# Forming the input projection of an S5 / RG-LRU layer with seven block products in place of eight

## The chip, the cores and the metric

The kernel runs on one core of one Trainium2 chip. The metric is the device time of one execution in microseconds (us). The engines are TensorE (PE in the profile, with its weight loads as PEld), VectorE (DVE), ScalarE (ACT), GpSimd (POOL) and SyncE (SP, which here only issues DMAs). The matmul accumulators lie in PSUM, in banks of 128 x 512 float32.

## The reference, cut to what matters

2048 tokens of a prompt and 128 of eight samples (2176 in all) pass through one layer of width 1024:

```python
h = rmsnorm(x, ln_g)
proj = h @ w_in                                   # 1024 -> 5120 columns
u_a, z_a, u_b, z_b, g_a, g_b = split(proj)        # 512, 512, 1024, 1024, 1024, 1024
y_a, s5_new = s5_mixer(u_a, ...)                  # complex diagonal scan, 32 groups
y_a = gelu(y_a); y_a = y_a * sigmoid(y_a @ w_glu + b_glu)
p_a = (y_a * silu(z_a)) @ w_pa
xc, conv_new = causal_conv(u_b, ...)              # width 4
y_b, lru_new = rglru(xc, ...)                     # gates, then a scan over the tokens
p_b = (y_b * silu(z_b)) @ w_pb
m = sigmoid(g_a) * p_a + sigmoid(g_b) * p_b
out = rmsnorm(x + m @ w_out, final_gain)
```

The input projection `h @ w_in` is by far the largest product.

## The kernel before

Tokens lie in five tiles, four of 512 and one of 128 (the samples); features lie over the partitions, in blocks of 128. Every large product is made in float16 pairs: a float32 operand is split into a high and a low part (`wsplit` for weights: an ACT copy, then a DVE subtraction), and `gemm` (lines 172 to 178) makes three passes for each of the eight blocks of the contraction: high by high, high by low, low by high. A column block of 128 by a token tile of 512 is so 24 matmuls of 512 columns. The normalised, transposed input `hT` stays on chip for the whole run, and each of the 40 column blocks of `w_in` is loaded once, split once (the class `Stream`, two raw buffers and three split ones) and multiplied with all five token tiles.

The stages follow one another, and in each the helper calls are written out in the order in which the engines run them:

- **P1** (to about 125 us): RMSNorm, transposes, the columns `u_a`; meanwhile the parameters of the S5 branch are made, and go to memory (`parD`, `uD`, SP and GpSimd queues).
- **Stage B** (125 to 545): eight blocks b. Each makes the columns UB and ZB over the five tiles, and beside them the convolution (`xc`), the block-diagonal gate products (`xs`, `wbs`), the scan (`q`, line 752) and y_b, split for the next product.
- **P4B** (545 to 966): eight blocks m, each with the columns of gate B and the projection `w_pb`. Between its tiles stand 54 "visits", the steps of the S5 branch (16 pairs of groups: building matrices on DVE, small matmuls, a scan, the result to memory as `yDp`).
- **Stage A** (966 to about 1115): reload of the S5 result (`ya`, split into `yh`), the columns `z_a`, the GLU product (`gl`, `qz`, `yA`).
- **P4A** (to about 1385): the columns of gate A, the projection `w_pa`, the merge.
- **Output projection** (lines 1332 to 1334), residual, final norm, to the end.

Helper lines: `stt` 66, `tt` 54, `act` 75, `ts` 70 and 72. So one line in the profile stands for many places, and the names of the tiles tell them apart.

Of the kernel before, what the change touches and what calls it, by code (L numbers as in the profile page):

```python
# [17 lines left out]
P = 128  # L18
# [11 lines left out]
# column starts of the combined input projection  # L30
C_UA, C_ZA, C_UB, C_ZB, C_GA, C_GB = 0, 512, 1024, 2048, 3072, 4096

# power-of-two scales of the fp16 (high, low) parts
# [9 lines left out]
# per-pair parameter record of the S5 branch (float32 words per partition)  # L43
# [5 lines left out]
def build(tc, I, O):  # L49
# [30 lines left out]
    with ExitStack() as es:  # L80
# [5 lines left out]
        def ps(tag, shape=(P, 512)):  # L86
            bufs = {"mm": 4, "a": 2, "b": 2}[tag]
            return psp.tile(list(shape), F32, tag=tag, name="ps_" + tag, bufs=bufs)

# [24 lines left out]
        mbD = dr.tile([8, P, T], F32, name="mbD")  # L114

# [10 lines left out]
        class Stream:  # L126
            def __init__(self, jobs):
                self.jobs, self.raw, self.sp, self.nl, self.ns = jobs, {}, {}, 0, 0

            def load(self):  # L130
                if self.nl < len(self.jobs):
                    src, nk = self.jobs[self.nl]
                    r = wp.tile([P, KB, P], F32, tag="wraw", name="wraw", bufs=2)
                    SP.dma_start(out=r[:, 0:nk], in_=src)
                    self.raw[self.nl] = r
                    self.nl += 1

            def split(self):
                if self.ns < len(self.jobs):
                    w = wp.tile([P, KB, 2, P], F16, tag="wsp", name="wsp", bufs=3)  # L140
                    wsplit(w, self.raw.pop(self.ns), self.jobs[self.ns][1])
                    self.sp[self.ns] = w
                    self.ns += 1

            def step(self):
                """splits the next block and starts the load two further on."""
                while self.nl < min(self.ns + 2, len(self.jobs)):
                    self.load()
                self.split()
                while self.nl < min(self.ns + 2, len(self.jobs)):  # L150
                    self.load()

            def take(self, i):
                while self.ns <= i:
                    self.step()
# [1222 lines left out]
```

## Time and profile before

| | |
|---|---|
| runs shown | 1559.58 and 1561.09 us, median 1560.34 |
| profiled execution, span | 1562.1 us |
| PE busy | 1509.9 us, 97% of the span |
| DVE busy | 886.2 us, 57% |
| ACT busy | 632.9 us, 41% |
| POOL busy | 170.5 us, 11% |
| moved by DMA | 115.99 MB, mean 74 GB/s |

A row "out<-in xcount | busy, mean ns | idle before <-releaser" is a group of like instructions; the idle time is that of the engine just before them. A PE row lasts longer than the time between two starts, since matmuls overlap; the cost of a matmul is read from the starts.

### The profile page before, as it was taken

How to read it: one execution, taken by the hardware profiler on the slowest of the kernel's cores; microseconds unless marked ns; L12 is line 12 of the kernel's file. 1: busy time of each engine (PE TensorE's matmuls, PEld its weight loads, DVE VectorE, ACT ScalarE, POOL GpSimd, SP SyncE). 2: the span in 40 equal slices, each digit the busy share in tenths (PEclk: the TensorE clock that was granted, in tenths of full speed). 3: DMA queues.
4: the chain of work that ended last, by engine and by line, in shares of the span. 5: the costliest groups of instructions: out<-in, count | busy, mean ns of one | idle time of the engine just before them, and what ended most of it. 6: DMA issues, size and time to landing. Idle time of an engine off the chain costs nothing.

```text
span 1562.1 us, 22054 instructions
## 1 busy us (share of the span) xinstructions
PE 1509.9 (97%) x8552; PEld 759.2 (49%) x8552; DVE 886.2 (57%) x1841; ACT 632.9 (41%) x1204; POOL 170.5 (11%) x344
## 2 busy tenths in 40 slices
PE   7999999999999999999999999979999999999998
PEld 4544444444444445555555554435444444444444
DVE  6557688878888775566655411864623320473333
ACT  7544465456545624444444311742322221242222
POOL 0780000000000003122222210000000000220000
PEclk9999999999999999999999999989999999999999
DMA  8298010101000123323333222231211210352331
GB/s 205 92 98 198 14 29 16 29 14 29 16 27 14 41 71 91 100 84 89 104 90 105 61 62 70 78 103 50 91 50 49 78 49 14 109 168 94 108 108 68
DMA packets 133458, 115.99 MB, mean 74 GB/s; under 512 B 35146, under 2 KB 112602, under 8 KB 132840
## 3 DMA queue, kind: packets, MB, share of 16 engines
q1 hardware_dynamic: 126056, 95.65, 23.4%
q0 software_dynamic: 7296, 18.92, 3.8%
q8 instruction: 67, 1.10, 0.3%
q14 instruction: 39, 0.32, 0.1%
HBM read 83.01 MB, written 31.53 MB: 73 GB/s over the span
## 4 chain that ended last, share of the span: by engine, by line
PE 68%; DVE 18%; ACT 8%; issue 2%; DMA 2%; POOL 1%; SPq 0%; POOLq 0%; DVEq 0%; ACTq 0%
PE ps_mm L176 17%; PE ps_mm L177 17%; PE ps_mm L178 17%; PE ps_mm L1333 4%; PE ps_mm L1334 4%; PE ps_mm L1332 4%; DVE xc L66 3%; DVE q L752 2%; ACT L75 1%; DVE sz L54 1%; ACT yh L75 1%; DVE q L54 1%; DVE wo L66 1%; ACT wsp L75 1%; PE ps_a L932 1%
## 5 line engine op out<-in xcount | busy, mean ns | idle before, releaser
L176 PE MATMUL ps_mm<-hT,wsp 128*128 128x512 f16 (+1 forms) x1440 | 486.2, 347 | 2.2 <-DVE qz L66 1.9
L177 PE MATMUL ps_mm<-hT,wsp 128*128 128x512 f16 (+1 forms) x1440 | 486.7, 347 | 0.0
L178 PE MATMUL ps_mm<-hT,wsp 128*128 128x512 f16 (+1 forms) x1440 | 485.7, 347 | 0.0
L177 PEld LDWEIGHTS <-wsp 128*128 128x128 f16 x2000 | 195.9, 98 | 198.6 <-issue 14.6
L176 PEld LDWEIGHTS <-wsp 128*128 128x128 f16 x2000 | 195.9, 98 | 191.6 <-issue 6.5
L178 PEld LDWEIGHTS <-wsp 128*128 128x128 f16 x2000 | 195.9, 98 | 189.5 <-issue 1.1
L66 DVE SCALAR_TENSOR_TENSOR wsp<-wraw,wsp 128x1024 f16<-128x1024 f32 (+1 forms) x56 | 62.0, 1108 | 111.2 <-ACT wsp L75 110.5
L176 PE MATMUL ps_mm<-y,wsp 128*128 128x512 f16 (+1 forms) x320 | 108.2, 347 | 0.0
L178 PE MATMUL ps_mm<-y,wsp 128*128 128x512 f16 (+1 forms) x320 | 108.2, 347 | 0.0
L177 PE MATMUL ps_mm<-y,wsp 128*128 128x512 f16 (+1 forms) x320 | 108.2, 347 | 0.0
L1333 PE MATMUL ps_mm<-wo,m 128*128 128x512 f16 (+2 forms) x280 | 104.1, 373 | 0.2 <-DVE wo L66 0.2
L1332 PE MATMUL ps_mm<-wo,m 128*128 128x512 f16 (+2 forms) x280 | 104.1, 373 | 0.0
L1334 PE MATMUL ps_mm<-wo,m 128*128 128x512 f16 (+2 forms) x280 | 104.0, 373 | 0.0
L1125 POOL DMA_DIRECT2D mbD<-gb x40 | 22.0, 551 | 663.6 <-DVE gb L66 663.5
L66 DVE SCALAR_TENSOR_TENSOR xc<-ub,PC,xc 128x512 f32<-128x512 f32 (+1 forms) x120 | 80.6, 672 | 4.2
L75 ACT ACTIVATE ga<-ps_mm 128x512 f32<-128x512 f32 (+1 forms) x40 | 21.2, 532 | 123.5 <-PE ps_mm L178 123.5
L75 ACT ACTIVATE gb<-ps_mm 128x512 f32<-128x512 f32 (+1 forms) x40 | 21.2, 530 | 121.0 <-PE ps_mm L178 90.8
L66 DVE SCALAR_TENSOR_TENSOR ga<-ga,ps_mm 128x512 f32<-128x512 f32 (+1 forms) x40 | 24.1, 602 | 79.2 <-PE ps_mm L178 78.8
L75 ACT ACTIVATE jk<-xo 128x512 f16<-128x512 f32 (+2 forms) x35 | 21.6, 617 | 109.5 <-DVE xo L66 109.5
L66 DVE SCALAR_TENSOR_TENSOR xo<-ps_mm,xo 128x512 f32<-128x512 f32 (+2 forms) x35 | 23.6, 675 | 71.0 <-PE ps_mm L1334 71.0
L75 ACT ACTIVATE y<-sz 128x512 f16<-128x512 f32 (+1 forms) x40 | 22.6, 566 | 94.3 <-DVE sz L54 94.3
L75 ACT ACTIVATE xs<-xc 128x512 f16<-128x512 f32 (+1 forms) x40 | 22.6, 566 | 90.7 <-DVE xc L66 90.7
(260 smaller groups left out, 2345.1 us busy)
## 6 DMA issues: line engine op xcount, KB each, us to landing
wraw<-w_in SPq DMA_DIRECT2D x40, 512.0 KB, 4.0
xt<-x_prompt SPq DMA_DIRECT2D x16, 512.0 KB, 4.2
mbD<-gb POOLq DMA_DIRECT2D x32, 256.0 KB, 2.3
ya<-yDp SPq DMA_DIRECT2D x32, 256.0 KB, 4.5
mb<-mbD SPq DMA_DIRECT2D x32, 256.0 KB, 4.2
xo<-x_prompt SPq DMA_DIRECT2D x16, 512.0 KB, 4.5
o_y_prompt<-xo SPq DMA_DIRECT2D x16, 512.0 KB, 2.9
uD<-uE POOLq DMA_DIRECT2D x4, 1088.0 KB, 11.4
```

Of the source, the lines that this page charges most:

```text
L54: V.tensor_tensor(out=out, in0=a, in1=b, op=op)
L66: V.scalar_tensor_tensor(out=out, in0=a, scalar=s, in1=b, op0=op0, op1=op1)
L75: S.activation(out=out, in_=a, func=f, **kw)
L176: PE.matmul(p, lhsT=W[:, k, 0], rhs=xh, start=(k == 0), stop=False)
L177: PE.matmul(p, lhsT=W[:, k, 0], rhs=xl, start=False, stop=False)
L178: PE.matmul(p, lhsT=W[:, k, 1], rhs=xh, start=False, stop=(k == nk - 1))
L752: V.tensor_tensor_scan(out=q, data0=a, data1=q, initial=0.0 if n == 0 else prev[:, w - 1:w], op0=MUL, op1=ADD)
L932: PE.matmul(o[:, 16 + P * j:16 + P * j + w], lhsT=lb, rhs=d["wc"][:, j, g].rearrange("p (h t) -> p t h", t=8)[:, 0:w // 16], start=True, s ...
L1125: G.dma_start(out=mbD[m, :, t0:t0 + w], in_=g)
L1332: PE.matmul(p, lhsT=lh[0], rhs=wo[:, k, 0, c], start=(k == 0), stop=False)
L1333: PE.matmul(p, lhsT=lh[0], rhs=wo[:, k, 1, c], start=False, stop=False)
L1334: PE.matmul(p, lhsT=lh[1], rhs=wo[:, k, 0, c], start=False, stop=(k == KB - 1))
```

## The change

All column blocks of the input projection but `u_a` and the first two of gate B are made in pairs: 17 pairs, in the order b0, gate B 2, b1, gate B 4, ..., b7, and two pairs of `z_a`; the pair of b is (UB, ZB) of the same b. For two column blocks and two token tiles (a "quad") the weights are a 2 x 2 block matrix A (column block by half of the contraction) and the input is a 2 x 2 block matrix B (half of the contraction by token tile). Seven products of sums of these blocks give the four results, where eight would be needed directly. The sample tile is made directly. The sums of the input (`T1` to `T4`, `t_forms`) are formed once, on DVE, and kept; those of the weights (`S1` to `S4`, `w_forms`) are formed for each pair. Between the products, partial sums in PSUM are copied out or added (`b_after`, `g_after`).

```diff
+        def t_forms(j):
+            for k in range(4):
+                def whole(q, n):
+                    t = gt([P, 512], name="hw")
+                    s = HQ[q, n][:, k]
+                    tt(t, s[:, 0], s[:, 1], ADD)
+                    return t
+                def parts(i, t):
+                    d = TF[i, j][:, k]
+                    scopy(d[:, 0], t)
+                    tt(d[:, 1], t, d[:, 0], SUB)
+                b12, b11 = whole(0, b), whole(0, a)
+                yield 1.2
+                b22 = whole(1, b)
+                tt(b11, b12, b11, SUB)
+                parts(1, b11)
...
+        PROD = [("A11", "11", "X", 1), ("S1", "T1", "Z", 1), ("S2", "T2", "X", 0), ("A12", "21", "Y", 1),
+                ("S3", "T3", "X", 0), ("S4", "22", "Z", 0), ("A22", "T4", "X", 0)]
+        def quad(W, j, after, hook):
...
+            for i, (a, b, z, first) in enumerate(PROD):
+                if first:
+                    bank[z] = ps("mm")
+                A, B = form(W, a), rhs[b]
+                for k in range(4):
+                    passes(bank[z], A[:, k], B[:, k], first == 1 and k == 0, k == 3, not first)
+                after[i](bank[z])
+                hook()
...
+            def snap(z):
+                def f(b):
+                    e[z] = gt([P, 512], name="gs")
+                    scopy(e[z], b)
+                return f
+            def total(z, m, n):
+                def f(b):
+                    tt(e[z], b, e[z], ADD)
+                    gate(kind, m, n, e[z], e[z])
+                return f
...
+        W0 = page_b("w", (2, 8, 2, P), "wf")
+        for i in range(2):
+            wsplit(W0[:, i], raws[i], KB)
+        raw = load_pair(0)
...
+        for n in range(NT):
+            for i in range(2):
+                p = proj(lambda k: W0[:, i, k], n)
+                t = wt(n, name="gs")
+                act(t, p, AF.Tanh, scale=0.5 / WS)
+                store(gbD, i, n, t)
...
+                if n == NT - 2:
+                    drain(tg[0])
+                    next(wg)
+                    next(wg)
```

What else moves:

- **Memory.** `W0` lies in a pool (`page_b`) laid over the memory that P1 gives back. The split of UB's first block lay in a buffer of its own.
- **Gates and y.** The tanh of both gates, silu of `z_a` and y_b go to memory (`gbD`, `gaD`, `zaD`, `ybD`, GpSimd queue) and are loaded again (SP queue) where they are used.
- **Branch B** for block b is cut into tasks, issued a piece at a time behind the products of its own pair and of the gate pair that follows.
- **S5 visits** no longer stand between gate-B and `w_pb` tiles. Some stand in the last two pairs; most stand in P4B, which now is only the projection `w_pb`, tile by tile of tokens (32 units of 24 matmuls, with 40 visits); eight visits follow after P4B.
- **The tail** goes by token tile: for each, `glu_prep` (split of the S5 result), `ga_tile` (GLU, `w_pa`, merge), then `out_tile`; the first two of tile n+1 are issued between the pieces of `out_tile` of tile n.
- **PSUM**: five buffers for large products and three for the rest, before four, two and two. ACT's table loads are 72 in number, before 24.

The places where the order changes most, as the built programs have it. First ACT, at the end of P1, before:

```order
L75 ACTIVATE wsp<-wraw 128x8x128 [waits DMAHW6_49]
L75 ACTIVATE ub<-ps_mm 128x512 [waits PE_49]
L75 ACT_TABLE_LOAD
L75 ACTIVATE pt<-ps_a,HB 128x512 [waits PE_49]
L75 ACTIVATE q<-ps_b,HB 128x512 [waits PE_49]
L75 ACTIVATE xs<-xc 128x512 [waits DVE_49,Activation_49]
L75 ACTIVATE a<-pt,SPL 128x512 [waits DVE_49]
```

The same place on ACT now; `wf` is `W0`, the first weights of the next stage, `gs` a gate tile, `T` a form of the input:

```order
L75 ACTIVATE uE_119<-ps_mm 128x8x32 [waits PE_49]
L75 ACTIVATE uE_119<-ps_mm 128x8x32
L75 ACTIVATE wbs<-wbd 128x2x128
L75 ACTIVATE wf<-wraw 128x8x128 [waits DMAHW0_49,DMAHW1_49,DMASW4_49,DMAHW2_49,DMASW3_49,DMAHW3_49,DMASW2_49,DMAHW4_49,DMASW1_49,DMAHW5_49,DMASW0_49,DMAHW6_49,DVE_49,DMAHW7_49,Activation_49,Pool_49]
L75 ACTIVATE wf<-wraw 128x8x128
L75 ACT_TABLE_LOAD
L75 ACTIVATE gs<-ps_mm 128x512 [waits PE_49]
L75 ACTIVATE T_1432<-hw 128x512 [waits DVE_49]
```

Before, UB's first weights waited for their own load alone. Now the first split waits for every queue that P1 used: it is the first instruction to write the memory that P1 leaves, and the last transfers on these queues that read it are `parD<-m16c` (SP) and the last `uD<-uE` (GpSimd).

Then DVE, from the first split of the forms of a pair's weights (`wf<-wraw`, after 27 of the 32 forms `T`) to the second:

```order
L54 TENSOR_TENSOR T_1635<-hw,T_1635 128x512 [waits Activation_49]
L66 SCALAR_TENSOR_TENSOR wf<-wraw,wf 128x4x128 [waits DMAHW7_49,PE_49,Activation_49]
L54 TENSOR_TENSOR wt<-wraw 128x512 [waits DMAHW0_49]
L66 SCALAR_TENSOR_TENSOR wf<-wt,wf 128x4x128 [waits Activation_49]
L54 TENSOR_TENSOR hw<-h_103 128x512
L54 TENSOR_TENSOR hw<-hw 128x512 [waits DVE_49]
L54 TENSOR_TENSOR T_1637<-hw,T_1637 128x512 [waits Activation_49]
L54 TENSOR_TENSOR hw<-h_102 128x512
```

These rows stand in a new place: nothing like them was there before. The forms `T` come ahead of the weights of the first quad on DVE, and in each of them the low part waits for ACT's copy of the high part.

Last PE, at the end of P4B, now (`Y,wpb` is the last tile of the projection, the `L12..` rows are S5 steps, `yh,wgl` is the first GLU product; some 200 S5 rows lie between the two parts shown):

```order
L155 MATMUL ps_mm<-Y,wpb 128x128
L164 MATMUL ps_a<-ident,wb 128x128 x4
L1198 MATMUL ps_a<-par 32x16
L1201 MATMUL ps_a<-wc,par 32x128
...
L1293 MATMUL ps_a<-u,d_11714 128x272
L153 LDWEIGHTS wgl
L153 MATMUL ps_mm<-yh,wgl 128x512
```

Before, columns of `z_a` stood between the last S5 steps and the first product with `yh`; now there is no large product between them.

## Rows read from the trace of the kernel before

**Rows 1.** the page: engine, busy us, share of the span, instructions.
```profile
PE 1509.9 (97%) x8552; PEld 759.2 (49%) x8552; DVE 886.2 (57%) x1841; ACT 632.9 (41%) x1204; POOL 170.5 (11%) x344
```

**Rows 2.** waits of PE: row, releaser: idle us in total, times, longest.
```profile
PE ps_mm L176 <- DVE qz L66: 12.4, 3, 9.3
PE ps_a L176 <- ACT xs L75: 9.2, 14, 0.7
PE ps_a L177 <- DVE xs L54: 5.8, 14, 0.5
...
PE ps_b L188 <- DMA rows<-state_lru: 3.1, 1, 3.1
```

**Rows 3.** stages: stretch, us, PE, PEld, DVE, ACT, POOL busy, PEclk, DMA, GB/s.
```profile
125.00:545.00 420.00, 401.86 (x2163) 193.52 (x2162) 334.82 (x616) 229.26 (x405) 0.53 (x1) 1.00 0.14 36
545.00:966.00 421.00, 421.00 (x2764) 228.98 (x2762) 219.36 (x579) 153.65 (x337) 82.22 (x140) 1.00 0.27 82
```

**Rows 4.** timeline of PE in P4A: start us, us, instruction; 27 starts apart.
```profile
1301.13 0.38 PE L176 MATMUL ps_mm<-hT,wsp 128*128 128x512 f16 x1
...
1306.96 0.38 PE L176 MATMUL ps_mm<-hT,wsp 128*128 128x512 f16 x1
```

**Rows 5.** timeline of PE, the first product of stage B.
```profile
124.49 0.38 PE L176 MATMUL ps_mm<-hT,wsp 128*128 128x512 f16 x1
```

**Rows 6.** timeline of the SP queue around the end of P1.
```profile
124.60 12.60 SPq L544 DMA_DIRECT2D parD<-m16c  x1
```

**Rows 7.** timeline of ACT: what follows in stage B.
```profile
148.13 0.60 ACT L75 ACTIVATE ub<-ps_mm 128x512 f32<-128x512 f32 x1 [1.48 <-DMA parD<-m16c]
```

**Rows 8.** groups on ACT: shapes, count | busy us, mean ns | idle before, releaser.
```profile
L75 ACT ACTIVATE wsp<-wraw 128x1024 f16<-128x1024 f32 x44 | 46.0, 1045 | 0.1
L75 ACT ACTIVATE yh<-ya 128x256 f16<-128x256 f32 x32 | 36.4, 1502 | 21.4 <-DMA ya<-yDp 21.4
...
L75 ACT ACT_TABLE_LOAD x24 | 30.8, 1283 | 1.2 <-PEq L1369 0.7
...
L75 ACT ACTIVATE gl<-ps_mm,HB 128x512 f32<-128x512 f32 x16 | 10.7, 671 | 4.6 <-PE ps_mm L178 4.6
...
L75 ACT ACTIVATE yA<-qz 128x512 f16<-128x512 f32 x16 | 10.1, 629 | 33.7 <-DVE qz L66 31.6 <-issue 2.1
```

**Rows 9.** busy time around the longest PE wait.
```profile
1020.00:1025.00 5.00, 0.00 (x0) 0.00 (x0) 4.96 (x6) 5.00 (x7) 0.00 (x0) 0.50 0.39 138
1025.00:1030.00 5.00, 4.90 (x12) 1.72 (x12) 5.00 (x7) 5.00 (x10) 0.00 (x0) 0.50 0.00 0
```

**Rows 10.** timeline of PE after that wait, seven starts apart.
```profile
1026.33 0.63 PE L176 MATMUL ps_mm<-yh,wsp 128*128 128x512 f16 x1
...
1029.32 0.63 PE L177 MATMUL ps_mm<-yh,wsp 128*128 128x512 f16 x1
```

**Rows 11.** groups on DVE, in the same columns.
```profile
L66 DVE SCALAR_TENSOR_TENSOR wsp<-wraw,wsp 128x1024 f16<-128x1024 f32 x44 | 53.8, 1223 | 69.4 <-ACT wsp L75 68.7 <-PE ps_a L188 0.6
...
L54 DVE TENSOR_TENSOR yh<-ya,yh 128x256 f16<-128x256 f32 x32 | 36.3, 1325 | 18.0 <-ACT yh L75 18.0
...
L66 DVE SCALAR_TENSOR_TENSOR gb<-gb,ps_mm 128x512 f32<-128x512 f32 x32 | 21.8, 683 | 61.8 <-PE ps_mm L178 61.8
...
L66 DVE SCALAR_TENSOR_TENSOR gl<-gl,ya 128x256 f32<-128x256 f32 x32 | 17.5, 593 | 5.7 <-ACT gl L75 5.7
...
L54 DVE TENSOR_TENSOR yA<-qz,yA 128x512 f16<-128x512 f32 x16 | 11.1, 692 | 11.8 <-ACT yA L75 11.8
```

**Rows 12.** timeline of DVE in stage B: one operation behind another.
```profile
144.81 0.69 DVE L66 SCALAR_TENSOR_TENSOR q<-q,xc 128x512 f32<-128x512 f32 x1
145.41 0.69 DVE L54 TENSOR_TENSOR xs<-xc,xs 128x512 f16<-128x512 f32 x1
```

**Rows 13.** DMA issues: count, KB each, median us to landing.
```profile
ya<-yDp SPq DMA_DIRECT2D x32, 256.0 KB, 4.5
...
yDp<-yo POOLq DMA_DIRECT2D x32, 128.0 KB, 3.3
```

## What the change should do to the time

> **What bounds the kernel now.** The engine table comes first: PE is busy 97% of the 1562.1 us span, DVE 57%, ACT 41% [rows 1]. PE's own waits come next, to see how much of its idle time anything could give back: the four largest come to some 30 us, of which 12.4 wait for DVE before the GLU product and 15 for the split of `xs` in stage B [rows 2]. So the kernel is one long queue on PE, and time is saved there by fewer columns or not at all. The windows by stage then say how much cover the other engines have left: in stage B DVE works 334.8 us of 420, in P4B 219.4 of 421 [rows 3]. A change that takes work from PE and gives it to DVE spends this cover, so the stages are gone through one by one.
>
> **A. Columns removed: -88.** A quad needs 7 products of 12 matmuls for 8. The projection's matmuls of 512 columns go from 3456 to 3048: 17 pairs x 2 quads x 12 = 408 fewer. 27 starts take 5.83 us, 0.216 us each [rows 4]; 408 x 0.216 = 88.1. All of it is on the path, since PE is the path. The 128-wide tile is unchanged.
>
> **B. First weights behind P1's transfers: +24 (18 to 27).** PE went from P1 straight into UB, at 124.49 [rows 5], because its weights had a buffer of their own. `W0` lies over P1's memory, and its split waits for the last transfers out of it. Such a wait is in the trace: `parD<-m16c` is issued from 124.60, an issue of 12.6 us [rows 6], and ACT's `ub`, whose buffer likewise lies where P1's were, went on at 148.13 [rows 7]. PE did not feel it then. Now the high split follows (1.05 [rows 8]), so PE starts at 149.2 and stands still for 24.7. From this goes the 3.1 us wait for `state_lru` that stood there [rows 2]. After a long idle PE runs slowly: after the wait that ended at 1025 the granted clock was 0.50, the lower level, and twelve matmuls started 0.427 apart [rows 9, 10] (2.99 us for seven) instead of 0.216, which is 2.5 us. 24.7 - 3.1 + 2.5 = 24.1. The lower end is a transfer that lands some 6 us earlier because SP's queue has less ahead; a gain is excluded, since nothing in P1 gets shorter.
>
> **C. Forms of the input ahead of the first quad: +39 (10 to 45).** `W0` gives PE two column blocks: 8 x 24 x 0.216 = 41.4 and 2.7 for the small tiles, 44.1, so it covers until 149.2 + 2.5 + 44.1 = 195.8. Meanwhile DVE, from 151.5 (two more splits of 1.2 behind ACT's [rows 8, 11]), must finish 27 forms before it splits the first weights of quad 0. Each costs a whole (0.69) and a difference, ACT's copy and the low part. The nearest row for that handover is `yA`: the low part takes 0.69, and DVE idles 11.8 / 16 = 0.74 before it [rows 11]. Behind one another, operations of this size start 0.60 apart [rows 12]. With 0.60 to 0.69 for the difference and the low part that is 1.95 to 2.1 us, and 0.60 to 0.69 for the whole; 27 x 2.55 = 69 to 27 x 2.8 = 76. DVE ends at 220 to 227, the first weights 2 later; taken is 224. PE idles 28 (2.5 for the clock), then about 9 at `S2`, whose split stands behind five further handovers. Sum 39. If ACT's copies ran ahead of DVE (no idle), the chain would be 27 x 3 x 0.6 = 49 and the idle 7: hence the 10.
>
> **D. The pairs: +5 (0 to 20).** A pair of b takes PE 44.4 us (2 quads of 84 matmuls, 2 x 24 small ones, 24 gate matmuls and six small ones), a gate pair 38.9; 83.3 together. On DVE such a period holds the block of branch B (334.8 / 8 = 41.9 [rows 3]), less two splits, plus weight forms of two pairs (24 operations of 0.69, 17), plus sums of snapshots (8 to 10): 64 to 70. ACT: 229 / 8 = 29, two pairs of copies (16 x 0.63), snapshots, gates and four table loads, about 57. So cover remains, and PE waits only at the products whose bank is still being read, 1 to 2 us a period, against 15 us of `xs` waits that go or stay [rows 2].
>
> **E. P4B: +5 (0 to 25).** Now 32 units of 24 matmuls (166 us) carry 40 visits. DVE's 219.4 in P4B [rows 3] less gates (21.8) and 16 splits (19.6 [rows 11]) is 178, 11 per pair of groups, which is 3 visits. PE's 421 less 64 x 24 x 0.216 and 16 small tiles of 1.3 leaves 68, 4.3 per pair of groups. So PE has 166 + 40/3 x 4.3 = 223 and DVE 147 for S5, 22 for the merge, 22 for the split of y, 16 for weights: 207. Nearly balanced, where before it was half.
>
> **F. S5 steps behind P4B: +17 (10 to 28).** Eight visits run with no large product beside them: 8/3 x 11 = 29 if DVE sets the pace, then `yDp` stored 3.3, `ya` loaded 4.5 [rows 13], `yh` split (2 x 1.50 on ACT and 1.33 on DVE [rows 8, 11]) 4.3: 41 us, of which PE works 11.5. Idle 30, and 2.5 for the clock, against 12.4 and 2.5 before at the same place [rows 2, 10]. Lower end: the first steps overlap the last, small tiles of P4B; upper: each step also waits for ACT and DMA.
>
> **G. The tail: +15 (8 to 28).** Tile 0 has nothing beside it: after the last GLU product come tanh 0.67, two products of 0.59, one of 0.69, a copy of 0.63 and the low part 0.69 [rows 8, 11], 4.5 with the handovers, before `w_pa`. Tiles 1 to 3 lie beside the output projection, but ACT and DVE hold the splits of `yh` in order behind the residual and the norm: 3 to 4 each. Seventeen table loads are in the tail (before, one), at 1.28 us [rows 8]; eight of them lie ahead of a tanh that PE waits for, and are in the 15. The Trainium skill, "ScalarE: Activation LUTs", section "Step-by-step: what each stage is for", puts a table load at about 2.7 us with the drain; by that this term would be 26 and the whole 1588, an estimate. The trace's 24 loads disagree, so the row's price is used.
>
> Stores and reloads of gates and y are taken at nothing: 28 blocks of 128 x 2176 float32 are some 31 MB out and 31 MB in, the DMA engines are busy 0.14 of the time in stage B and 0.27 in P4B [rows 3], and the loads are issued two tiles ahead. If that cover goes, a load of some 4 us, as `ya` [rows 13], shows at a tile.
>
> Sum: -88 + 24 + 39 + 5 + 5 + 17 + 15 = +17. Lower ends: -88 + 18 + 10 + 0 + 0 + 10 + 8 = -42. Upper: -88 + 27 + 45 + 20 + 25 + 28 + 28 = +85. The profiled span, 1562.1, stands 1.8 above the median of 1560.3; taken as a difference, the sum gives 1577 (1518 to 1645).
>
> **The rivals.**
>
> *The savings show (faster), 0.27.* The forms are made while `W0` runs, and S5 and the tail are covered. It decides at C: if DVE and ACT run the chain back to back, with the 0.60 us spacing, C falls from 39 to 10, and with the lower ends of the others 1518 comes out. For it: DVE had free time in every stage. Against it: DVE idles for ACT in each of the rows that have the same handover.
>
> *DVE becomes the bound in the pairs (slower), 0.30.* In a period of 83.3 us DVE has 64 to 70 of work and 24 handovers from ACT; each that is not filled costs the 0.74 us of `yA` [rows 11], 17 us, which brings DVE to 81 to 87, and the small waits of the snapshots tip it. From there each of the eight periods is as long as DVE's chain: 5 to 8 us more, 40 to 64 in all, and 1577 + 50 = 1627. For it: before, DVE's idle times lie exactly in front of such low parts. Against it: the tasks of branch B are interleaved, so another instruction can fill the gap. The Trainium skill, "Trainium Kernel Development and Optimization", section "Best Practices", warns that evacuating PSUM does not get faster when TensorE's part does; no run here shows yet whether it binds, and it speaks for this rival.
>
> *The forecast as summed, 0.43:* most of the gain is given back at the opening, the S5 end and the tail.
>
> **Numbers.** Within 2% (1529 to 1592, about what a measurement of this kernel can tell from no change) lies the forecast, with its upper end outside: a part of it, 0.03, and the second rival make slower 0.33; faster 0.27; within 2% 0.40. The range from 1512 to 1632 takes in both rivals' values and leaves out the far ends.
>
> **What would show it.** PE idle from 124.5 to about 149 and again from about 196 to 224, with the granted clock at 0.50 after each, would bear out B and C; matmuls of the projection 0.216 apart and 12 per product bear out A. D and E show as PE waits for DVE between 225 and 1150; F as a stretch of some 40 us with only S5 matmuls. Wrong would be: PE over 95% busy in the first 225 us (C and B), or PE waits in the pairs over 40 us in all (D).

## The result: slower by about 10%

The changed kernel takes 1711.3 us (median of 1707.36 and 1715.24) where the kernel before takes 1560.34: a ratio of 1.0971, interval 1.0908 to 1.1033. The forecast was 1577, the range ended at 1632, and the slower rival stood at 1627. Its mechanism, DVE as the bound in the pairs, is not what happened either.

The page of the changed kernel answers to [rows 1]: the span is 1705.6 us, and PE is busy 1473.7 us, less than before, but in 86% of the span only.

```profile
PE 1473.7 (86%) x8144; PEld 737.1 (43%) x8144; DVE 1100.8 (65%) x2216; ACT 798.9 (47%) x1448; POOL 224.6 (13%) x469
```

PE's waits after, beside [rows 2] (line waited for; us in total, times, longest). There, four rows came to 30 us. Here the first five alone come to 138, and no row of before answers to them:

```profile
PE ps_mm L153 <- ACT wf L75: 46.4, 2, 29.6
PE ps_mm L153 <- ACT Y L75: 33.4, 4, 11.8
PE ps_mm L153 <- ACT gs L75: 21.2, 2, 11.8
PE ps_a L1286 <- ACT d L75: 19.9, 3, 7.9
PE ps_a L1286 <- DVE wbT L66: 17.2, 6, 5.5
PE ps_mm L153 <- DVE gs L54: 12.0, 16, 2.5
PE ps_mm L153 <- ACT ub L75: 11.5, 1, 11.5
...
PE ps_a L164 <- DVE h L66: 9.4, 6, 2.9
```

`wf` and `ub` belong to the opening, `gs` from ACT to the end of the pairs, `wbT` and three of the four `Y` stops (23.1 us) to P4B, `h` to P1. The fourth `Y` stop (10.3) and two of the three `d` stops (14.6 of 19.9) lie behind P4B's large tiles. The windows by stage, in the columns of [rows 3], show where PE stands still:

```profile
125.00:150.00 25.00, 7.96 (x35) 3.10 (x34) 3.74 (x9) 4.02 (x8) 1.59 (x3) 0.75 0.88 222
150.00:196.00 46.00, 46.00 (x236) 21.71 (x237) 31.34 (x50) 12.86 (x21) 2.71 (x5) 0.95 0.14 47
196.00:226.00 30.00, 0.48 (x9) 0.31 (x6) 21.58 (x35) 9.02 (x15) 1.08 (x2) 0.55 0.07 26
226.00:250.00 24.00, 12.41 (x37) 4.57 (x38) 17.25 (x29) 9.12 (x19) 1.60 (x3) 0.64 0.12 39
250.00:925.00 675.00, 656.86 (x3632) 320.77 (x3631) 475.42 (x853) 373.83 (x642) 61.22 (x114) 1.00 0.19 63
925.00:1003.00 78.00, 52.66 (x270) 24.63 (x268) 45.18 (x86) 26.48 (x46) 8.08 (x15) 0.85 0.41 128
1003.00:1310.00 307.00, 241.70 (x1477) 131.74 (x1476) 202.79 (x513) 132.99 (x288) 68.97 (x118) 0.89 0.49 157
1310.00:1354.00 44.00, 25.76 (x299) 22.18 (x299) 18.03 (x60) 16.08 (x39) 14.22 (x24) 0.75 0.26 73
1354.00:1706.00 352.00, 325.02 (x1564) 148.77 (x1563) 217.28 (x417) 144.36 (x240) 1.06 (x2) 0.96 0.36 126
```

Rows 1 to 4 are the opening, row 5 the pairs, row 6 the last two pairs, row 7 P4B with the first of the sample tile, row 8 the rest of that tile and the S5 steps behind it, row 9 the tail. Two prices are in such a row: PE's idle time, and the clock. PE's busy time is also longer where the granted clock is below 1.00. The table below adds them from windows of 2.5 us (idle, and busy x (1 - granted clock)), against the stage that held the same work before; its P4B goes from 1002.5 to 1302.5, the row after it to 1352.5. The forecast's terms stand beside it.

| stage | idle + clock, us | before | difference | forecast |
|---|---|---|---|---|
| P1 | 20.2 + 1.7 | 15.6 | +6 | 0 |
| opening, 125 to 250 | 58.2 + 7.1 | 0 | +65 | B, C: +63 |
| pairs, 250 to 925 | 18.1 + 0.0 | 18.1 | 0 | D: +5 |
| last two pairs | 25.3 + 5.7 | 0 | +31 | 0 |
| P4B | 57.8 + 16.7 | 0 | +75 | E: +5 |
| S5 behind P4B | 24.3 + 5.6 | 15.1 | +15 | F: +17 |
| tail | 28.1 + 11.3 | 7.3 | +32 | G: +15 |

The sum is +224; less the 88 us of columns it is +136, where the spans differ by 143.5. The 7 that remain lie in PE's busy time: less the clock's share it fell from 1505.9 to 1425.4 us, by 80 and not 88. The mean granted clock fell from 0.995 to 0.939: 48 us of the 1706 are lost by it, before 4. They are lost in stretches of some 3 to 11 us at the lower level (0.50, 1.2 GHz): from 125 us on, behind each of the 15 stops of 4.7 to 29.6 us and, in the tail, behind groups of shorter ones. Behind the single stops of up to 2 us in the pairs, 18.1 us together, the clock stayed at 1.00.

### The profile page after: what moved, and what is told of

The parts are those of the page before. It is cut to its first block, busy times and chain, and to the rows that moved or that the text cites. A ratio compares the mean times of both kernels' runs of the same rounds, so it can differ in the third digit from the quotient of the medians.

```text
span 1705.6 us, 22380 instructions
## 1 busy us (share of the span) xinstructions
PE 1473.7 (86%) x8144; PEld 737.1 (43%) x8144; DVE 1100.8 (65%) x2216; ACT 798.9 (47%) x1448; POOL 224.6 (13%) x469
## 5 line engine op out<-in xcount | busy, mean ns | idle before, releaser
L153 PE MATMUL ps_mm<-T,wf 128*128 128x512 f16 x544 | 209.0, 384 | 45.0 <-ACT gs L75 21.2
L153 PE MATMUL ps_mm<-h,wf 128*128 128x512 f16 x472 | 181.3, 384 | 46.4 <-ACT wf L75 46.4
L155 PE MATMUL ps_mm<-T,wf 128*128 128x512 f16 x544 | 209.2, 385 | 0.0
L154 PE MATMUL ps_mm<-T,wf 128*128 128x512 f16 x544 | 209.2, 385 | 0.0
L153 PEld LDWEIGHTS <-wf 128*128 128x128 f16 x1304 | 128.4, 98 | 176.5 <-ACT wf L75 55.1
L154 PEld LDWEIGHTS <-wf 128*128 128x128 f16 x1304 | 128.5, 99 | 161.8 <-issue 48.0
L155 PEld LDWEIGHTS <-wf 128*128 128x128 f16 x1304 | 128.5, 99 | 124.6 <-issue 5.2
L154 PE MATMUL ps_mm<-h,wf 128*128 128x512 f16 x472 | 180.9, 383 | 0.0
L155 PE MATMUL ps_mm<-h,wf 128*128 128x512 f16 x472 | 180.4, 382 | 0.2 <-DVE wf L66 0.2
L153 PE MATMUL ps_mm<-Y,wpb 128*128 128x512 f16 (+1 forms) x320 | 112.4, 359 | 33.4 <-ACT Y L75 33.4
L154 PE MATMUL ps_mm<-Y,wpb 128*128 128x512 f16 (+1 forms) x320 | 111.7, 357 | 3.3 <-DVE Y L54 3.1
L155 PE MATMUL ps_mm<-Y,wpb 128*128 128x512 f16 (+1 forms) x320 | 111.4, 356 | 0.0
L1664 PE MATMUL ps_mm<-wo,M 128*128 128x512 f16 (+2 forms) x280 | 104.6, 375 | 0.0
L1665 PE MATMUL ps_mm<-wo,M 128*128 128x512 f16 (+2 forms) x280 | 104.6, 375 | 0.0
L1666 PE MATMUL ps_mm<-wo,M 128*128 128x512 f16 (+2 forms) x280 | 104.5, 375 | 0.0
L66 DVE SCALAR_TENSOR_TENSOR wf<-wraw,wf 128x512 f16<-128x512 f32 (+1 forms) x87 | 60.8, 700 | 65.7 <-ACT wf L75 65.7
L75 ACT ACT_TABLE_LOAD x72 | 92.4, 1283 | 2.0 <-PEq L1722 0.7
L66 DVE SCALAR_TENSOR_TENSOR xc<-ub,PC,xc 128x512 f32<-128x512 f32 x96 | 72.2, 752 | 3.4
L75 ACT ACTIVATE wf<-wraw 128x512 f16<-128x512 f32 (+1 forms) x87 | 55.1, 634 | 25.2 <-DMA rows<-state_conv 14.7
L66 DVE SCALAR_TENSOR_TENSOR wf<-wt,wf 128x512 f16<-128x512 f32 x51 | 35.3, 692 | 45.0 <-ACT wf L75 45.0
L75 ACT ACTIVATE gs<-ps_mm 128x512 f32<-128x512 f32 (+1 forms) x92 | 48.1, 532 | 26.7 <-PE ps_mm L155 26.6
```

What stands on the lines that cost most here:

```text
L66: V.scalar_tensor_tensor(out=out, in0=a, scalar=s, in1=b, op0=op0, op1=op1)
L75: S.activation(out=out, in_=a, func=f, **kw)
L153: PE.matmul(p, lhsT=a[:, 0], rhs=b[:, 0], start=first, stop=False, skip_group_check=more)
L154: PE.matmul(p, lhsT=a[:, 0], rhs=b[:, 1], start=False, stop=False, skip_group_check=more)
L155: PE.matmul(p, lhsT=a[:, 1], rhs=b[:, 0], start=False, stop=last, skip_group_check=more)
L1664: PE.matmul(p, lhsT=lh[0], rhs=w_[:, 0, c], start=(k == 0), stop=False)
```

## Where the time goes, stage by stage

**The opening went as forecast.** The timeline of PE (start, us, instruction, idle before): the start of `W0` (forecast 149.2), the first product of quad 0 (forecast 224) and the product with `S2`:

```profile
148.69 0.61 PE L153 MATMUL ps_mm<-h,wf 128*128 128x512 f16 x1 [16.82 <-ACT wf L75]
...
226.07 0.61 PE L153 MATMUL ps_mm<-h,wf 128*128 128x512 f16 x1 [29.59 <-ACT wf L75]
...
244.59 0.59 PE L153 MATMUL ps_mm<-T,wf 128*128 128x512 f16 x1 [11.52 <-ACT ub L75]
```

The first wait is 16.8 us and not 24.7, since P1's products now run to 131.9, where before the next stage began at 124.49 [rows 5]. The profile puts the wait of ACT's first split (147.58) down to `rows<-state_conv`, a load that stands behind `parD<-m16c` in SP's queue; `parD<-m16c` itself, issued at 126.79 and landed after 20.4 us, is there at 147.2. Either would do, and no run separates them. The start is not a constant either: `W0` starts at 155.8 to 158.7 in the profiles of the seven other kernels below with this P1, and at 147.1 to 151.3 in the eight with four small PSUM buffers, whose P1 is shorter. The third is put down to `ub`, the copy that frees the bank of the `S2` product: it stands in ACT's queue behind the split of the `S2` weights, as term C had it. The handover of the forms is what `yA` in [rows 11] priced at 0.74: on DVE `T` idles 26.3 us in all, 4.77 before the first and 0.69 on the mean before each of the other 31.

```profile
L54 DVE TENSOR_TENSOR T<-hw,T 128x512 f16<-128x512 f32 x32 | 22.2, 693 | 26.3 <-ACT T L75 26.3
```

**The last two pairs** were not in the forecast. The end of a pair needs ACT to copy partial sums out of PSUM (`gs`). First SP's queue, then ACT's, then PE's, in three views:

```profile
975.47 7.67 SPq L1406 DMA_DIRECT2D wraw<-w_pb  x3
983.19 1.52 SPq L1438 DMA_DIRECT2D yr<-ybD  x3
```

```profile
987.21 0.63 ACT L75 ACTIVATE Y<-yr 128x512 f16<-128x512 f32 x1 [5.72 <-DMA yr<-ybD]
987.74 0.58 ACT L75 ACTIVATE gs<-ps_mm 128x512 f32<-128x512 f32 x1
```

```profile
988.37 0.58 PE L153 MATMUL ps_mm<-T,wf 128*128 128x512 f16 x1 [11.80 <-ACT gs L75]
```

P4B's first weights and the first y are loaded and split while the last pair still runs. The copy `gs` stands behind the split of `Y` in ACT's queue, `Y` behind a load, the load behind 7.7 us of issues and waits for the buffers of `wraw`: 11.8 us on PE for a copy of 0.58. In the other `gs` stop (9.4 us, to 947.24) S5's first matrices stand in that place: ACT waits 10.4 us for DVE's `wc`.

**P4B**, the 32 units of the large tiles, takes from 1004.7 to 1298.5, 294 us, where 223 were forecast. (The expectations of the experiments count from the end of the wait above, 988.4, to the end of a wait in the sample tile, 1310.2: 322 us. That stretch holds 16 us of the last pair, 1.3 us of sample products and a stop of 10.3.) DVE is busy 202.8 of the 307 us in the window, so it has 104 to spare, and yet PE waits for it. The timeline of DVE shows how; PE's row of the same time stands in the fence after it:

```profile
1204.75 0.75 DVE L54 TENSOR_TENSOR t<-par 128x256 f32<-128x256 f32 x2
1205.54 0.69 DVE L54 TENSOR_TENSOR wc<-wc,t 128x512 f32<-128x512 f32 x1
1206.98 0.69 DVE L66 SCALAR_TENSOR_TENSOR wcs<-wc,wcs 128x512 f16<-128x512 f32 x1 [0.76 <-ACT wcs L75]
1207.59 0.68 DVE L54 TENSOR_TENSOR Y<-yr,Y 128x512 f16<-128x512 f32 x1
1208.45 1.23 DVE L66 SCALAR_TENSOR_TENSOR wo<-wraw,wo 128x1024 f16<-128x1024 f32 x1 [0.17 <-ACT wo L75]
1209.59 0.68 DVE L66 SCALAR_TENSOR_TENSOR gb<-gb,ps_mm 128x512 f32<-128x512 f32 x1
1210.19 0.68 DVE L66 SCALAR_TENSOR_TENSOR wbT<-ps_a,wbT 128x512 f16<-128x512 f32 x1
```

```profile
1210.93 0.41 PE L1286 MATMUL ps_a<-u,d 128*128 128x272 f16 x1 [5.49 <-DVE wbT L66]
```

PE waits 5.49 us for a split of 0.68. The matmul does not read `wbT`; it needs the small PSUM buffer that this split empties. DVE had just made the matrices of a later group (`wc`) and then had the split of y, of `w_out` and the merge ahead of it. The engine is not full; the one instruction that PE needs stands behind others in its queue.

SP's queue couples the stages too. S5 stores a small matrix and loads it again (`dd<-kpD`), and until the store has landed SP issues nothing else. SP's waits for that from 988 to 1310, then one stop traced from SP over ACT to PE, in three timelines:

```profile
SPq L1215 <- DMA kpD<-kh: 127.9, 13, 14.5
```

```profile
1145.51 2.45 SPq L1215 DMA_DIRECT2D dd<-kpD  x4
1149.68 0.44 SPq L1406 DMA_DIRECT2D wraw<-w_pa  x1
1155.46 0.63 ACT L75 ACTIVATE wpa<-wraw 128x512 f16<-128x512 f32 x1 [9.25 <-DMA wraw<-w_pa]
1165.01 0.61 ACT L75 ACTIVATE Y<-yr 128x512 f16<-128x512 f32 x1
1165.67 0.58 PE L153 MATMUL ps_mm<-Y,wpb 128*128 128x512 f16 x1 [10.86 <-ACT Y L75]
```

ACT stands 9.25 us at the split of `w_pa`, whose load was issued behind the reload, and S5 steps and the split of `Y` follow in ACT's order. Before, SP waited 192 us for the same stores in P4B, but only weights and S5's own loads stood behind them, and PE never stopped; now the loads of y and of the gates do too. No run varied this.

**Behind P4B and in the tail** the mechanism was in the main the forecast one. First the sample tile's products stop for 10.3 us, to 1310.16, for the split of their y, which stands behind P4B's last visits in ACT's queue. From the last of these products (1322.3) to the first with `yh` (1354.55) are 32.3 us of S5 steps and reload (forecast 41). Then come `yh` and `yA` waits in each tile. The table loads cost what [rows 8] showed, and ACT hardly idles before them:

```profile
L75 ACT ACT_TABLE_LOAD x72 | 92.4, 1283 | 2.0 <-PEq L1722 0.7
```

## Experiments

Each was timed against the kernel before on the same chip (1560.1 to 1560.9). The change itself stands at a ratio of 1.097.

**1. Is the saving real?** The product into `Y` is done twice, so that each quad has its eighth product again (408 matmuls; the second time over the first, so the result is the same).

```diff
-                for k in range(4):
-                    passes(bank[z], A[:, k], B[:, k], first == 1 and k == 0, k == 3, not first)
+                for _ in range(2 if z == "Y" else 1):
+                    for k in range(4):
+                        passes(bank[z], A[:, k], B[:, k], first == 1 and k == 0, k == 3, not first)
```

> One of the seven products of each quad is made twice (the second time over the first, so the result is the same): 34 x 12 = 408 matmuls of 512 columns more, as many as the change took away. Theory: PE sets the pace in the pairs and the saving is there in full, so it costs 408 x 0.216 = 88 us: 1790 to 1800. Rival: DVE and ACT set the pace in the pairs, and most of it hides: under 1760.

1784.33 us (1780.17 to 1789.02), ratio 1.1437 [1.1411, 1.1462]: 73 of the 88 us come back, between the two expectations. PE sets the pace in the pairs, and DVE is not the bound there. Most of the other 15 went into the short waits of the first 15 pairs: in the two profiles PE's waits there are 29.4 and 17.7 us, in the last two pairs 25.3 in both.

**2. Do the two terms of the opening add?** The second block of `W0` is not multiplied (gate B's block 1 takes the product of block 0), so the cover ahead of quad 0 is halved.

```diff
             for i in range(2):
-                p = proj(lambda k: W0[:, i, k], n)
+                if i == 0:
+                    p = proj(lambda k: W0[:, 0, k], n)
```

> The changed kernel without the product for the second column block of gate B (the first block's product is used in its place): 22 us of PE work less between P1 and the first quad, all else as it was. Theory: the first quad waits for the forms of the input on DVE, whose chain starts when P1's transfers have landed; PE only idles longer before it, and the time stays within 3 us of the changed kernel's: 1705 to 1714. Rival: the two idle times add up, each behind the work before it, and 22 us come off: 1685 to 1692.

1714.24 us (1710.73 to 1716.35), ratio 1.0981 [1.0959, 1.1004]. The wait before quad 0, by the timeline of PE, is 22.0 longer than in the change, and the end does not move:

```profile
233.34 0.61 PE L153 MATMUL ps_mm<-h,wf 128*128 128x512 f16 x1 [51.63 <-ACT wf L75]
```

22 us of large products there are worth nothing. From the start of `W0` to quad 0 are 76.5 us (in the change 77.4) whatever PE does in between: the chain of forms behind the first split sets when quad 0 begins. B and C are one chain, cut in two where PE works on `W0`.

**3. Is that chain made of handovers?** The low part of a form is written behind the next difference, so that ACT's copy has time.

```diff
-                tt(b12, b22, b12, SUB)
-                parts(3, b12)
+                tt(b12, b22, b12, SUB)
+                copy(3, b12)
+                low(1, b11)
...
```

> The forms of the input are made in another order on DVE: the low part of a form stands behind the next difference, so that ACT's copy runs beside it; the same operations. Theory: the first quad waits for the chain of 32 forms, in which DVE idles 0.69 us for each of the copies; some 27 of these go, the first quad starts at about 208 instead of 226, and the time falls by 15 to 20, to 1691 to 1696. Rival: the first quad waits for something else (the weights' load, ACT's queue), and it starts within 4 us of 226: 1707 to 1715.

1702.11 us (1700.79 to 1706.68), ratio 1.0914 [1.0893, 1.0935]. Quad 0 starts 49.8 us after `W0` (it was 77.4), and the long wait is gone:

```profile
205.54 0.39 PE L153 MATMUL ps_mm<-h,wf 128*128 128x512 f16 x1 [2.55 <-ACT wf L75]
```

So the handovers are the 28 us, as term C said. But only 9 reach the end, between the two expectations. From quad 0 to the stop in the last pair it now takes 775 us for 762: 13 us of what PE no longer waits for at quad 0 it waits for in the first pairs. And in this profile `W0` starts 7 us later than in the change's, at 155.8.

**4. What stops P4B: the splits of y?** They stand behind the visits; here they go ahead of them.

```diff
                 if n < NT - 1:
+                    y_step()
                     visit()
                     if m % 4 == 3:
                         visit()
-                    y_step()
```

> In P4B each unit now issues its split of a block of y ahead of its one or two S5 visits instead of behind them; nothing else differs from the changed kernel (1711). Theory: the last block of the next token tile's y is split in the unit that carries two visits, behind them in ACT's and DVE's order, so PE waits 10 to 12 us at the start of each token tile (33.4 us in four waits on ACT's Y) and then runs at the lower clock. The waits on Y fall under 6 us, and with the clock 35 to 45 us come back: 1666 to 1676. Rival: the chain of S5 steps on DVE and ACT sets P4B's pace, and what is taken from the waits on Y comes back as waits on d, wbT and kf: 1695 to 1711.

1708.61 us (1705.46 to 1712.63), ratio 1.0955 [1.0928, 1.0981]: no change, as the rival had it. The `Y` waits (33.4) are gone and the others have grown; P4B takes 288 us for 294. PE's waits:

```profile
PE ps_a L1286 <- DVE wbT L66: 28.4, 8, 6.0
PE ps_a L1286 <- ACT d L75: 24.1, 5, 7.9
```

**5. Or the three small PSUM buffers?** Four and four for five and three.

```diff
-            bufs = {"mm": 5, "a": 3}[tag]
+            bufs = {"mm": 4, "a": 4}[tag]
...
```

> PSUM is shared out as four buffers for the large products and four for the rest, instead of five and three. Theory: the S5 matmuls wait for a free one of the three small buffers (17.2 us on DVE's wbT, 4.7 on kf, the transposes in P1 9.4 on h), which before had four; these waits fall by about 20 us together and the time to 1685 to 1695. Rival: the waits are for the data of the S5 steps, and stay; the pairs lose 1 to 2 us each with one buffer less: 1711 to 1735.

1691.88 us (1690.59 to 1693.14), ratio 1.0843 [1.0827, 1.0859]: 20 us back, as the theory had it. In P4B, now 283 us, it is 11: the waits for `wbT` go from 17.2 to 7.5, `Y` stays at 32.9. The `h` waits of P1's transposes (9.4) are gone, P1 is shorter and `W0` starts at 147.1, which against the 155.8 to 158.7 of the other kernels is worth some 9. The Trainium skill, "Perfetto Trace Analysis", section "Optimization Strategy", says that the same gap recurring on an engine that ought to be full can mean too little PSUM for the next tile; this run agrees, with 20 us for one more small buffer (and one large one less).

**6. Both.**

> Both edits at once: four and four PSUM buffers, and in P4B the split of y ahead of the S5 visits. Theory: alone, the second only turned waits on y into waits for a free small PSUM buffer; together both go, P4B falls from 322 us to 285 or less, and the time to 1665 to 1675. Rival: the chain of S5 steps, one waiting for the other across PE, ACT and DVE, sets P4B's pace whatever stands around it: within 5 us of the run with the PSUM buffers alone, 1687 to 1697.

1679.95 us (1676.98 to 1682.7), ratio 1.0763 [1.0744, 1.0782]: 31 us back where the two alone gave 20 and 3, between the two expectations. P4B takes 273 us, 21 less than in the change. The edit of 4 is worth 12 once a buffer is free. Experiments 8, 9 and 10 and the second of 11 start from this kernel.

**7. What does a visit cost without cover?** All visits stand behind P4B.

```diff
-                    visit()
-                    if m % 4 == 3:
-                        visit()
                     y_step()
```

> No S5 visit between the units of P4B; the 40 of them follow after P4B with the other eight. P4B alone is then some 40 units, 187 us. This prices a visit with nothing beside it. Theory: a visit is a chain of steps that wait for each other over three engines, 5.2 us each as in the eight behind P4B (41 us); 48 of them take 250 us, the time is 1790 to 1815, and P4B's 322 us are this chain with the products only partly beside it. Rival: DVE's work alone, 3.7 us a visit, sets the pace: 48 take 180 us, 1735 to 1750.

1793.5 us (1792.42 to 1794.58), ratio 1.1491 [1.1468, 1.1514], as the theory had it. Three visits repeat in 15.95 us, by the timeline of PE:

```profile
1199.73 0.39 PE L1286 MATMUL ps_a<-u,d 128*128 128x272 f16 x1 [2.86 <-DVE wbT L66]
...
1215.68 0.41 PE L1286 MATMUL ps_a<-u,d 128*128 128x272 f16 x1 [2.35 <-DVE wbT L66]
```

That is 5.32 us a visit with nothing beside it, where the forecast took 11 / 3 = 3.7 by DVE's sum. Forty visits are 213 us alone, the product is 166, together 379. In the change P4B takes 294: of 166 us of cover 85 overlap with S5, about half.

**8. Give P4B more cover.** From 6, half of each `w_pb` product is done twice (384 matmuls, 83 us; the half product is overwritten by the whole, so the result is the same).

```diff
+                if n < NT - 1:
+                    gemm(p, lambda k: W[:, k], lambda k: Y[n, k // 4][:, k % 4], 4)
                 gemm(p, lambda k: W[:, k], lambda k: Y[n, k // 4][:, k % 4], KB)
```

> As the run with both edits (1680), with 12 matmuls made twice in each of the 32 units of P4B (the first half of each product, overwritten by the whole): 384 matmuls, 83 us of PE work more, so that 7.8 us of product stand beside a visit's work as they did before. Theory: P4B waits for the chain of S5 steps, and the added work falls into these waits: the time rises by 25 to 50, to 1705 to 1730. Rival: PE's own work sets P4B's pace: the whole 83 show, 1760 or more.

1721.07 us (1717.34 to 1726.02), ratio 1.1032 [1.1005, 1.1059]: 41 more for 83, as the theory had it; P4B takes 318 us for 273. Half of what is added fits into the waits, and the `d` waits fall from 15.6 to 8.0. P4B is bound neither by PE alone nor by the S5 chain alone.

**9. Space the steps of a group.** From 6, `s5_pe2` and the steps behind it come one visit later.

```diff
-            at(v + 1, s5_pe2, q)
-            at(v + 2, s5_hst, q)
-            at(v + 2, s5_d2, q)
-            at(v + 4, s5_pe3, q)
+            at(v + 2, s5_pe2, q)
+            at(v + 3, s5_hst, q)
+            at(v + 3, s5_d2, q)
+            at(v + 5, s5_pe3, q)
```

> As the run with both edits (four and four PSUM buffers, y split first; 1680), with the S5 steps of a pair of groups one visit further apart: the step that needs a result stands two visits behind the one that makes it, so a unit of the product lies between. Same work, one visit more. Theory: 5.3 us a visit is the wait of a step for the one just before; with a unit between, the waits on wbT and d in P4B go and P4B falls from 302 us by 20 to 40; the time is 1640 to 1660. Rival: DVE's and ACT's work in their own order is what takes the time, and the waits reappear on other tiles: 1675 to 1690.

1742.48 us (1740.14 to 1743.64), ratio 1.1165 [1.1149, 1.1182]: 62 slower than 6, which neither theory expected; 58 of them lie in P4B, which takes 332 us. PE's waits:

```profile
PE ps_a L1286 <- ACT d L75: 44.5, 12, 9.6
PE ps_a L1198 <- ACT yo L75: 33.2, 6, 10.8
```

And ACT's from 1000 to 1325; in 6 the first of these is 27.8, 13, 3.9:

```profile
ACT wcs L75 <- DVE wc L54: 88.7, 10, 10.2
ACT wpa L75 <- DMA wraw<-w_pa: 28.3, 3, 10.1
```

The edit does more than space the steps. In the change the matrices (`s5_mats`) of one group share a visit with `s5_hst` and `s5_d2` of an earlier one, `s5_pe1` shares one with loads only, and `s5_pe2` shares one with `s5_pe3`. With the edit matrices, `s5_pe2` (which holds the scan) and `s5_pe3` all fall into one visit, `s5_pe1`, `s5_hst` and `s5_d2` into the next, and the third is empty. So DVE has the scan and the matrices behind one another, and ACT stands before `wcs` for them. And only the distance from `s5_pe1` to `s5_pe2` grew; `s5_hst` still follows one visit later. Whether spacing alone helps was not tested.

**10. One visit a unit.** From 6, 32 visits in P4B, 16 behind it.

```diff
-                    if m % 4 == 3:
-                        visit()
```

> As the run with both edits (1680), with one visit a unit at most: the second visit of every fourth unit is left to the end, where 16 visits run in place of eight. Theory: the two visits of one unit have no product between them, so PE waits there; P4B falls by more than the 43 us that eight visits more cost behind it: 1650 to 1668. Rival: a visit costs P4B what it costs anywhere, and the sum stays: 1674 to 1690.

1701.19 us (1698.83 to 1708.4), ratio 1.0909 [1.0882, 1.0936], 21 slower than 6 and above both expectations. P4B shrinks by 21 to 252 us, but the stretch from there to the first product with `yh` grows by 42, from 52 to 94: a visit moved out of P4B takes there 2.6 us off and costs 5.2 behind it.

**11. The other two.** In the last pairs the first S5 steps come one visit behind their loads and the first two blocks of y are loaded earlier (on the change itself); and four steps of the next tile instead of two at the start of each tile of the tail (on 6):

```diff
-                s5_open()
+                if not opened:
+                    opened.append(1)
+                    s5_open()
+                    return
...
-            while len(yraw) < min(2, len(yjobs) - ydone):
+            while len(yraw) < min(1, len(yjobs) - ydone):
...
+                    y_load()
```

> In the last two pairs the first S5 loads are issued one visit ahead of the first use, and the first two blocks of y are loaded some products ahead of their split. Theory: PE's two waits for ACT's snapshots there (9.4 and 11.8 us, with the lower clock after each) come from ACT and DVE standing at a load issued just before; both go, and the time falls by 15 to 25, to 1686 to 1696. Rival: ACT then stands at the next load or at DVE's S5 work in the same place: under 8 us, 1703 or more.

1708.11 us (1705.05 to 1710.55), ratio 1.0943 [1.0924, 1.0962]. The `gs` waits fall from 21.2 to 12.5, the end by 3, within the scatter of the two kernels.

```diff
-            for _ in out_tile(n):
-                next(nxt, None)
-                next(nxt, None)
+            for i, _ in enumerate(out_tile(n)):
+                for _ in range(2 if i else 4):
+                    next(nxt, None)
```

> As the run with both edits (1680), with the four splits of the next tile's yh issued ahead of the first piece of the output projection's second row block instead of in two lots. Theory: PE's waits on yh and the lower clock behind them (in all three later tiles 2 us and four times 0.7 to 0.9) come from the splits standing too close before the product; issued a piece earlier they go, 8 to 12 us: 1668 to 1673. Rival: ACT works them off in its order behind the residual, and they are late as before: 1677 to 1684.

1683.43 us (1680.06 to 1689.02), ratio 1.0792 [1.0769, 1.0815]: no gain, as the rival had it. What the tail's remaining time is, beyond its `yh` and `yA` waits and the clock, stays open.

**12. S5 taken out of both kernels.** Zeros stand for the S5 result; loads, matrices, products and scans of S5 are left out.

```diff
...
-            at(v, s5_pe1, q)
-            at(v + 1, s5_pe2, q)
...
+            pass
```

> The kernel before without the steps of the S5 branch between its tiles (no building of matrices, no S5 matmuls, no scan; zeros go to memory as their result, and are read back and used as before). It prices these steps where they stood. PE spent 68 us on them: 1480 to 1495 if that was all they cost, as the full PE in that stage says.

The kernel before: 1494.45 us (1493.71 to 1495.06), ratio 0.9576 [0.9562, 0.9591]. S5 cost it 66 us, what PE itself does for it.

> The changed kernel without the same steps, zeros in place of their result. Theory: the place of the S5 steps (P4B, the eight visits behind it, the last two pairs) makes some 110 of the 151 us; without them the two kernels lie 25 to 50 apart, this one at 1510 to 1540, and what is left is the opening and the tail. Rival: the loss lies in the stages that are left, and S5 only shows it: 80 us or more apart, over 1565.

The change: 1530.66 us (1529.7 to 1532.53), ratio 0.981 [0.9796, 0.9825]. Without S5 the two are 36 us apart and not 151: 115 us come from what the change makes of S5's place. In the two profiles of the change, with S5 and without, P4B takes 294 and 170 us, the stretch from there to the first product with `yh` 56 and 11, and the pairs, from the first product with a form `T` to P4B, 774 and 752. PE's longest waits are then those of the opening:

```profile
PE ps_mm L153 <- ACT wf L75: 50.8, 2, 29.6
...
PE ps_mm L153 <- ACT ub L75: 11.6, 1, 11.6
```

**13. All that helped, together**: 3, 6, and the two edits of 11; then the same without the one in the tail.

> The edits that took something off, joined: four and four PSUM buffers, y split first, the forms of the input in the order that hides ACT's copies, the early loads of the last two pairs, the earlier split of yh. Theory: the losses lie in different places and add up: 1680 less 8 for the forms, 3 for the loads, 8 to 12 for yh: 1655 to 1663. Rival: what the forms gain is given back in the first pairs, as far as that showed before, and the others overlap: 1670 or more. In either case it stays behind the kernel before.

> The joined kernel (1669) without the earlier split of yh, which alone cost 3 us: 1660 to 1668 if the edits add up, 1669 or more if not.

1669.13 us (1665.05 to 1673.66), ratio 1.0701 [1.0675, 1.0727], just under the rival's 1670, and 1660.43 (1657.95 to 1662.38), ratio 1.0644 [1.0626, 1.0663], as forecast. The second is the best version of the change, 51 us under it and 100 over the kernel before, which no version with S5 in it beat. The two edits that it adds to 6 gave 9 and 3 us alone; on top of 6 they give 20 together.

## Why the prediction was wrong

- **A, columns: right.** Experiment 1 shows 73 of the 88, PE is the path where they were removed. By the traces PE's busy time at full clock fell by 80.
- **B and C, the opening: right in size** (65 for 63) **and in mechanism.** The split into two terms was an accident of the place of `W0`: experiment 2 shows one chain. That the size agrees so closely is in part luck: `W0` starts up to 10 us later in other profiles with the same P1. Of the rival "the savings show", experiment 3 tried the core: with the handovers filled the wait goes, but 13 of its 28 us come back in the first pairs.
- **D, the pairs: right.** PE's idle time there is 18.1 us, as in stage B before. The same product of two successive periods starts at 411.56 and 497.60 in PE's timeline: 86.0 us for the 83.3 worked out, of which 2.0 are two short waits. The rival "DVE becomes the bound" was given 0.30 and is wrong: DVE is busy 475 of 675.
- **E, P4B: the step that failed.** It set PE's 223 us against DVE's 207, called that nearly balanced, and allowed +5. It is +75 by the table; from first to last product P4B takes 294 us, 71 more than the 223. The step compared sums of busy time and took the longer for the stage, so a visit was to add PE's own 1.4 us (4.3 / 3) and no wait. It adds 3.1: P4B takes 170 us without the S5 steps and 294 with its 40 visits (experiment 12). Each S5 group is a chain across PE, ACT and DVE: alone a visit takes 5.32 us, not the 3.7 of DVE's sum (experiment 7). Every step stands in queues that also hold the splits of y, the weights and the merge, so PE waits 5.49 us for a split of 0.68 while DVE has a third of its time free. Before, a visit had 421 / 54 = 7.8 us of the stage and PE never stopped; now P4B takes 294 / 40 = 7.3 for each, of which only 166 / 40 = 4.1 are product. Of the 124 us between 170 and 294 the small PSUM buffer and the order of y are worth 21 (experiment 6). How the rest divides between the chain, the queues of DVE, ACT and SP, and buffers is not settled; S5 spread over the pairs, where there is cover, was not tried.
- **The last two pairs: left out.** The forecast moved loads and splits past the end of the pairs and costed them at nothing, though ACT's and SP's queues carry them ahead of `gs`: +31. The +6 of P1 is passed over too: its transposes share three small buffers, where there were two kinds of two, and their waits go with a fourth, and `W0` starts earlier (experiment 5).
- **F: right in size** (+15 for +17), in part by luck: the S5 steps alone cost less than forecast (32.3 us for 41), and some 8 of the row's 24 us of idle time are the sample tile's stop for `Y`, which the forecast did not have.
- **G: twice its size** (+32 for +15). Of it 21 is idle time and 11 the clock, which the forecast did not count there. The Trainium skill's larger price of a table load ("ScalarE: Activation LUTs", section "Step-by-step: what each stage is for"), weighed in the forecast (about 2.7 us with the drain), is not the reason: the 72 loads take 1283 ns on the mean, and ACT idles 2.0 us before all of them together.
- **The clock** was priced rightly for each long stop (2.5 us; the three of the opening cost 7.1), but most of the stops were not foreseen, those of 4.7 to 11.8 us in the last pairs and P4B and the groups of shorter ones in the tail: 48 us in all.

## What to carry to other kernels

Where a stage loses its cover, compare the latency of its dependent chain with the cover left for each step, and look up what stands ahead of each step in the in-order queues; sums of busy time per engine say only that it could fit. Waits that overlap do not add: taking one away (`Y`, the forms of the input) exposed the next. Work moved out of a well-covered stage has to be costed where it lands, with the clock behind its stops.

## What the runs showed that was not expected

- One PSUM buffer moved from large to small tiles is worth 20 us, about half of it through P1 and the start of `W0` (experiment 5), and it decides whether the order of the y splits matters at all (3 or 12 us).
- Steps moved apart by one visit made the kernel 62 us slower; the edit also bunched them (experiment 9).
- Three edits took away named waits of 9 to 33 us (`gs`, the forms, `Y`) and moved the end by 3 to 9 us; the first two gave more together than alone (experiment 13).
- A store and its reload in SP's queue hold up the loads of other stages, and through ACT's splits PE (the trace of P4B).
